# Token tile 0 leads at both changes of phase, and the convolution's inputs are computed with the activations stationary

## The chip, the cores and the metric

The kernel runs on one NeuronCore of a Trainium2 chip. The metric is the device time of one execution in microseconds (us). Its engines run apart from each other, each through its own list of instructions in order: TensorE (PE; the weight loads ahead of its matmuls are a row of their own, PEld), VectorE (DVE), ScalarE (ACT), GpSimd (POOL), and SyncE (SP), which here only issues DMA transfers. Semaphores join them.

## The reference

One residual block on 256 tokens of width 2048, batch 1, all in float32. It has three parts, each with an RMSNorm ahead and behind and with shift, scale and gate that come from a conditioning vector (9 x 2048 numbers out of a 2048 x 18432 matrix, the "ada" matrix):

```python
mod = jax.nn.silu(c) @ w_ada + b_ada                 # sh1, sc1, gt1, ..., gt3
h = modulate(rms_norm(x, g_pre[0]), sh1, sc1)
x = x + 0.5 * gt1 * rms_norm(swiglu(h, w_ffn1_gate, w_ffn1_up, w_ffn1_down), g_post[0])
h = modulate(rms_norm(x, g_pre[1]), sh2, sc2)
u_conv, q, k, v = split(h @ w_in)                    # 2048, 1024, 1024, 1024 columns
y_conv = conformer_conv(u_conv, ...)                 # a * sigmoid(g), 31 taps per channel, layer norm, silu
y_attn = diff_attention(q, k, v, ...)                # 8 heads, two softmaxes each
x = x + gt2 * rms_norm(concat([y_conv, y_attn]) @ w_out, g_post[1])
h = modulate(rms_norm(x, g_pre[2]), sh3, sc3)
x = x + 0.5 * gt3 * rms_norm(swiglu(h, w_ffn2_gate, w_ffn2_up, w_ffn2_down), g_post[2])
```

The feed-forward width is 5632. The convolution takes 2048 columns of w_in: 1024 values a and 1024 gates g.

## The kernel before

**Products.** The 256 tokens are two tiles of 128 (t = 0, 1), the 2048 channels 16 tiles (kt). A float32 product is three matmuls in the float32r format: each operand is split into a rounded part hi and a rest lo, and hi·hi, hi·lo and lo·hi are added in PSUM (mm3, L270 to L274). Weights come in blocks of 128 x 2048 floats (1 MB). `parts` (L156) loads one on the SP queue (four buffers), casts hi on ScalarE (L160) and subtracts lo on VectorE (L162); there are three hi and lo buffers. In an `s_tile` 128 x 128 pieces of the weights are stationary and 256 tokens move, so that the result has channels on the partitions; in an `m_unit` (L372) the activations are stationary (128 tokens) and 512 columns of weights move, and the result has tokens on the partitions.

**Ada chunks.** Each of the 144 chunks is 1 MB of the ada matrix: a load on the same queue and buffers, and one VectorE multiply-and-sum of 2.28 us (L183). They are strewn among the products; in ffn1 one comes per 1.1 weight blocks (EVERY1).

**Stages.** ffn1 (to about 774 us), mixing (to 1150), ffn2. Each starts with a front: `pre_norm` (L212) transposes the normalised x of both tiles for one channel tile (L218), applies scale and shift, splits, and the front adds that channel tile's products to all its open sums. In mixing the front is of class `Front` (weights stationary) and makes the first two of eight pairs (a, g) of conv channels; the other six pairs are twelve s_tiles (L638, L639). Sigmoid and gate follow (L641 to L647), then 31 taps per channel tile on VectorE (L627, L630). The taps wait in the list `fill`; each `parts` call takes up to 6 of them (TAPS), and what is left runs before the centering (`conv_done`). Then come the eight heads (q and k by s_tiles, softmax), two blocks of values, `mix_values` (L725 to L753) and `head_acts` (L760), and the four output blocks of w_out: the heads' half of the first three is done ahead while VectorE centers and normalises the conv channels (L789 to L818).

**Ends.** In the last products of each stage (`m_last`, L418) the third and fourth output blocks are run for token tile 0 first and then for tile 1. Weights of the third are split by pieces of 512 columns (`split_act`: L173 on ScalarE, L175 on VectorE). `evac` adds the partial sum (L486), ScalarE takes squares (L236), and L489 multiplies by the gate in place. `close` and `normed` then give the next stage's normalised x: L260, squares, L247.

**What sets the order.** The program only gives dependencies and hints (`behind`: not before the last matmul issued so far; `behind_dve`: the same for VectorE). The framework's scheduler puts each engine's instructions into one fixed order, and gives out the buffers (43 of 128 x 512 floats, called big).

## Time and profile before

| | |
|---|---|
| median of 3 runs | 1912.85 us (1911.74 to 1914.44) |
| the profiled execution's own time | 1911.84 us |
| its span | 1910.0 us |
| mean granted TensorE clock | 0.984 of full |
| TensorE busy | 1836.3 us (96%) |
| VectorE busy | 1423.6 us (75%) |
| ScalarE busy | 821.4 us (43%) |
| DMA | 492.58 MB, mean 258 GB/s |

Times in the views are us from the span's start. In a timeline a row has start, duration, engine, line, operation, result and operands, the count of like instructions in a row, and in brackets the idle time before it with what ended it. A matmul's duration holds the emptying of the pipeline; the rate is read from start to start. In the windows the columns are the window, its length, the busy time (and count) of PE, PEld, DVE, ACT and POOL, the granted TensorE clock (1.00 is 2.4 GHz, 0.50 is 1.2 GHz), the share of time that the DMA engines were busy, and GB/s. In the list of waits a row has the engine, the result and line that waited, what ended the wait, and then the sum, the number of waits and the longest.

### The profile page before, as it was taken

What the parts mean: (1) busy time and instruction counts of PE and PEld (TensorE: products, weight loads), DVE (VectorE), ACT (ScalarE), POOL (GpSimd) and SP (SyncE); (2) the same over time, 40 slices, a digit from 0 to 9 for tenths busy, and PEclk for the clock granted to TensorE, in tenths of its full rate; (3) what the DMA queues carried; (4) which work ended last, traced back from release to release, by engine and by line L of the source; (5) the groups of instructions that cost most, each with busy time, mean ns of one, the idle gap of its engine ahead of it and who ended that gap; (6) DMA issues with size and microseconds to landing.
All of it is one profiled execution on the core that took longest, in us unless ns stands there. A gap on an engine that the chain in (4) does not pass through costs nothing.

```text
span 1910.0 us, 22064 instructions
## 1 busy us (share of the span) xinstructions
PE 1836.3 (96%) x8944; PEld 1542.5 (81%) x8944; DVE 1423.6 (75%) x1594; ACT 821.4 (43%) x852; POOL 6.0 (0%) x49
## 2 busy tenths in 40 slices
PE   5999999999999999799998897999999999999997
PEld 3788888888888888699997686788888888888886
DVE  7789999788889888688998967854555555555455
ACT  4544445433433334643554454544344333343342
POOL 0000000000000000000000000000000000000000
PEclk9999999999999999899999898999999999999999
DMA  9888877989999998355444665865665666565552
GB/s 362 320 317 330 337 278 290 358 345 361 357 357 370 349 367 323 122 182 185 157 174 157 242 241 202 331 238 205 236 220 205 235 220 226 215 235 210 194 193 72
DMA packets 68934, 492.58 MB, mean 258 GB/s; under 512 B 7648, under 2 KB 7776, under 8 KB 9440
## 3 DMA queue, kind: packets, MB, share of 16 engines
q1 hardware_dynamic: 68832, 491.17, 69.0%
q8 instruction: 70, 1.15, 0.2%
q14 instruction: 32, 0.26, 0.0%
HBM read 489.05 MB, written 2.10 MB: 257 GB/s over the span
## 4 chain that ended last, share of the span: by engine, by line
PE 89%; DVE 5%; ACT 3%; DMA 2%; issue 0%; SPq 0%; DVEq 0%; ACTq 0%
PE ps L273 29%; PE ps L274 29%; PE ps L272 28%; DVE lo L162 2%; DMA raw<-in_wgu 2%; ACT hi L160 1%; DVE raw L183 1%; PE ps L413 1%; ACT tmp L236 1%; PE ps L312 0%; PE ps L311 0%; DMA raw<-in_wk 0%; PE ps L313 0%; PE ps L678 0%; PE ps L218 0%
## 5 line engine op out<-in xcount | busy, mean ns | idle before, releaser
L162 DVE TENSOR_TENSOR lo<-raw,hi 128x2048 fp32r<-128x2048 f32 x314 | 718.5, 2290 | 359.8 <-ACT hi L160 359.1
L160 ACT CAST hi<-raw 128x2048 fp32r<-128x2048 f32 x314 | 600.3, 1912 | 732.4 <-PE ps L274 362.0
L272 PE MATMUL ps<-hi,big 128*128 128x512 f32 x2256 | 879.2, 395 | 16.9 <-ACT big L227 11.3
L273 PE MATMUL ps<-lo,big 128*128 128x512 f32 x2256 | 884.0, 392 | 2.8 <-DVE lo L162 2.8
L274 PE MATMUL ps<-hi,big 128*128 128x512 f32 x2256 | 881.5, 392 | 2.0 <-DVE big L175 1.2
L272 PEld LDWEIGHTS ps<-hi,big 128*128 128x128 f32 x2256 | 426.1, 189 | 106.4 <-ACT big L227 12.7
L273 PEld LDWEIGHTS ps<-lo,big 128*128 128x128 f32 x2256 | 426.5, 189 | 92.5 <-DVE lo L162 6.2
L274 PEld LDWEIGHTS ps<-hi,big 128*128 128x128 f32 x2256 | 425.7, 189 | 92.5 <-DVE big L175 2.5
L183 DVE SCALAR_TENSOR_TENSOR raw<-raw,crow 128x2048 f32<-128x2048 f32 x144 | 327.7, 2283 | 0.6 <-DMA raw<-in_wada 0.5
L272 PE MATMUL ps<-big,hi 128*128 128x256 f32 x448 | 127.3, 284 | 0.0
L273 PE MATMUL ps<-big,hi 128*128 128x256 f32 x448 | 126.7, 283 | 0.0
L274 PE MATMUL ps<-big,lo 128*128 128x256 f32 x448 | 126.7, 283 | 0.0
L630 DVE SCALAR_TENSOR_TENSOR big<-big,par,big 128x256 f32<-128x256 f32 x240 | 100.1, 477 | 0.0
L272 PEld LDWEIGHTS ps<-big,hi 128*128 128x128 f32 x448 | 85.9, 192 | 0.3 <-issue 0.3
L273 PEld LDWEIGHTS ps<-big,hi 128*128 128x128 f32 x448 | 86.0, 192 | 0.0
L274 PEld LDWEIGHTS ps<-big,lo 128*128 128x128 f32 x448 | 85.9, 192 | 0.0
L397 ACT ACTIVATE tmp<-ps 128x256 f32<-128x256 f32 x64 | 24.3, 384 | 96.3 <-PE ps L274 96.3
L486 DVE TENSOR_TENSOR big<-ps,big 128x512 f32<-128x512 f32 x48 | 32.9, 691 | 31.7 <-PE ps L274 31.7
L358 DVE TENSOR_TENSOR big<-ps,big 128x512 f32<-128x512 f32 x72 | 45.2, 681 | 5.4 <-PE ps L274 5.4
L398 DVE TENSOR_TENSOR tmp<-ps,tmp 128x256 f32<-128x256 f32 x64 | 26.1, 421 | 30.9 <-ACT tmp L397 30.9
L218 PE MATMUL ps<-ident,big 128*128 128x128 f32 x96 | 19.7, 297 | 29.6 <-DVE big L247 28.7
L173 ACT CAST big<-ps 128x512 fp32r<-128x512 f32 x44 | 25.8, 585 | 38.0 <-PE ps L413 38.0
(135 smaller groups left out, 742.6 us busy)
## 6 DMA issues: line engine op xcount, KB each, us to landing
raw<-in_wada SPq DMA_DIRECT2D x144, 1024.0 KB, 6.1
raw<-in_wgu SPq DMA_DIRECT2D x116, 1024.0 KB, 5.0
raw<-in_wd SPq DMA_DIRECT2D x88, 1024.0 KB, 5.0
raw<-in_wk SPq DMA_DIRECT2D x60, 1024.0 KB, 5.5
raw<-in_wqk SPq DMA_DIRECT2D x28, 1024.0 KB, 4.8
raw<-in_wo SPq DMA_DIRECT2D x16, 1024.0 KB, 4.8
raw<-in_wv SPq DMA_DIRECT2D x8, 1024.0 KB, 4.8
raw<-in_wkc SPq DMA_DIRECT2D x4, 1024.0 KB, 5.1
```

Of the source, the lines that this page charges most:

```text
L160: nc.scalar.copy(hi, raw)
L162: ins = nc.vector.tensor_tensor(out=lo, in0=raw, in1=hi.bitcast(F32), op=ALU.subtract)
L173: nc.scalar.copy(hi[:, :w], v[:, :w])
L183: nc.vector.scalar_tensor_tensor(out=raw, in0=raw, scalar=1.0, in1=crow, op0=ALU.mult, op1=ALU.mult, accum_out=acc)
L272: nc.tensor.matmul(o, ah, bh, start=first, stop=False)
L273: nc.tensor.matmul(o, ah, bl, start=False, stop=False)
L274: last_mm[0] = nc.tensor.matmul(o, al, bh, start=False, stop=last)
L358: nc.vector.tensor_tensor(out=a[t], in0=b[t], in1=a[t], op=ALU.add)
L397: nc.scalar.activation(v[:, o], b[t][:, :S], AF.Silu)
L398: nc.vector.tensor_tensor(out=v[:, o], in0=b[t][:, S:], in1=v[:, o], op=ALU.mult)
L486: nc.vector.tensor_tensor(out=y[t][u], in0=b, in1=y[t][u], op=ALU.add)
L630: nc.vector.scalar_tensor_tensor(out=cot(c), in0=vps[c][:, j:j + S], scalar=w, in1=cot(c), op0=ALU.mult, op1=ALU.add)
```

## The change

- Conv inputs: mixing's front is now of the same class as the others (MFront, renamed Front): activations stationary, for the first two of four blocks of 512 columns (256 values a and their 256 gates). The other two blocks are m_units on a new array `wcv`. As the results have tokens on the partitions, `conv_block` copies them to SBUF, and `gated` transposes them (eight transposes a block) before sigmoid and gate. The s_tiles remain for q and k only.
- Entry: at both changes of phase pre_norm and the front run for token tile 0 alone over the first channel tiles (six in mixing, four in ffn2), then for tile 1 over the same, then for both over the rest. The first two transposes may be issued three products before the end of the last products (EARLY, LEAD).
- EVERY1 goes from 1.1 to 1.05; one `pop` more stands in the heads' loop.
- ffn's gate multiply writes into a new tile.
- Constants of mixing are set up ahead of ffn1's call.

```diff
-NF = (24, 2, 6)
+NF = (24, 4, 6)
...
-SET = (6, 2, 6)
+SET = (6, 4, 6)
 CUTS = (4, 8, 12, NK)
-EVERY1 = 1.1
+EVERY1 = 1.05
 TAPS = (3, 3, 3, 3)
...
+EARLY = 3
...
-    def pre_norm(l, xn, h, kt):
+    def pre_norm(l, xn, h, kt, ts=(0, 1)):
 
         b = bank()
-        for t in range(NT):
+        for t in ts:
             src = xn[t][kt // 4]
             o = (kt % 4) * P
             nc.tensor.transpose(b[:, t * P:(t + 1) * P], src[:, o:o + P], ident)
+        if len(h) == kt:
+            h.append(big(F32R))
+        both = h[kt]
+        o, e = ts[0] * P, (ts[-1] + 1) * P
         v = tmp()
         c = l * NK + kt
         if l and kt % 2 == 0:
-            nc.vector.tensor_scalar(out=v[:, :S], in0=b[:, :S], scalar1=gs[:, c:c + 1],
+            nc.vector.tensor_scalar(out=v[:, o:e], in0=b[:, o:e], scalar1=gs[:, c:c + 1],
                                     scalar2=sh[:, c:c + 1], op0=ALU.mult, op1=ALU.add)
         else:
-            nc.scalar.activation(v[:, :S], b[:, :S], AF.Identity, bias=sh[:, c:c + 1], scale=gs[:, c:c + 1])
-        both = big(F32R)
-        nc.scalar.copy(both[:, :S], v[:, :S])
-        last_dve[0] = nc.vector.tensor_tensor(out=both[:, S:], in0=v[:, :S], in1=both[:, :S].bitcast(F32),
-                                              op=ALU.subtract)
...
-        def step(self, kt, first, last):
+            self.banks = None
+            self.parts = {}
+
+        def step(self, kt, first, last, ts=(0, 1)):
             n = self.n
-            if first:
+            if first and ts[0] == 0:
                 self.banks = [[bank() for _ in range(NT)] for _ in range(n)]
             for j in range(n):
                 i = kt * n + j
-                if i % 4 == 0:
-                    self.parts = quarters(self.w[i // 4])
-                for t in range(NT):
-                    m_product(self.banks[j][t], t, (self.h[kt][:, :S], self.h[kt][:, S:]), self.parts[i % 4],
-                              first, last)
+                if i // 4 not in self.parts:
+                    self.parts[i // 4] = quarters(self.w[i // 4])
+                for t in ts:
+                    m_product(self.banks[j][t], t, (self.h[kt][:, :S], self.h[kt][:, S:]),
+                              self.parts[i // 4][i % 4], first, last)
...
-    def m_last(units, acts, after):
+    def m_last(units, acts, after, early=lambda: None):
...
+                    if t == NT - 1 and u == units[-1][0] and k == n - EARLY:
+                        early()
...
-                    nc.vector.tensor_tensor(out=y[t][u], in0=y[t][u], in1=gb[u], op=ALU.mult)
+                    yg = big()
+                    nc.vector.tensor_tensor(out=yg, in0=y[t][u], in1=gb[u], op=ALU.mult)
+                    y[t][u] = yg
                 if end and u == 3:
-                    xn.append(close(t, y, ss, 0.5, final))
+                    xn.append(close(t, y, ss, 0.5, nxt is None))
...
-                m_last([(u, srcs(u), None) for u in range(4 - N_LAST, 4)], acts, evac)
+                m_last([(u, srcs(u), None) for u in range(4 - N_LAST, 4)], acts, evac,
+                       (lambda: nxt.early(xn)) if nxt else (lambda: None))
...
+    class Entry:
+
+
+        def __init__(self, l, wk, late):
+            self.l, self.late = l, late
+            self.h = []
+            self.front = Front(wk, self.h, SET[l] // 2)
+            k0 = 4 * HI // self.front.n
+            self.items = [(kt, (t,)) for t in range(NT) for kt in range(k0)]
+            self.items += [(kt, (0, 1)) for kt in range(k0, NK)]
+            self.at = 0
+
+        def channels(self, xn):
+            if self.at < len(self.items):
+                kt, ts = self.items[self.at]
+                need([(3 * self.l, kt), (3 * self.l + 1, kt)], self.late)
+                pre_norm(self.l, xn, self.h, kt, ts)
+                self.at += 1
+
+        def early(self, xn):
+            for _ in range(LEAD):
+                behind(self.channels, xn)
+
+        def run(self, xn):
+            n_late = 0
+            for kt, ts in self.items:
+                self.channels(xn)
+                n_late += len(ts) / 2
+                while n_late >= LATE:
+                    n_late -= LATE
+                    behind_dve(next, self.late, None)
+                self.front.step(kt, kt == 0, kt == NK - 1, ts)
+            return self.h, self.front
...
+    mixing = Entry(1, wkc[0], bg)
+    xn = ffn(0, h, None, facts, wgu1, wd1, bg, EVERY1, mixing)
+
+
     need([(m, kt) for m in (3, 4) for kt in range(NK)], bg)
-    h, front = front_of(1, xn, wkc[0], iter(()))
+    mixing.late = iter(())
+    h, front = mixing.run(xn)
...
+    hacts = [(a[:, :S], a[:, S:]) for a in h]
+
+    def gated(cb, us):
+
+        ba, bg_ = bank(), bank()
+        for half, b in enumerate((ba, bg_)):
+            for j in range(2):
+                for t in range(NT):
+                    nc.tensor.transpose(b[:, j * S + t * P:j * S + (t + 1) * P],
+                                        us[t][:, half * S + j * P:half * S + (j + 1) * P], ident)
+        for j in range(2):
+            c = 2 * cb + j
+            js = slice(j * S, (j + 1) * S)
+            sg = tmp()
+            nc.scalar.activation(sg[:, :S], bg_[:, js], AF.Sigmoid,
+                                 bias=par[:, C_BIN + NC_ + c:C_BIN + NC_ + c + 1])
+            vp = big()[:, :S + KW - 1]
+            nc.gpsimd.memset(vp[:, 0:KW - 1], 0.0)
+            nc.vector.scalar_tensor_tensor(out=vp[:, KW - 1:], in0=ba[:, js],
+                                           scalar=par[:, C_BIN + c:C_BIN + c + 1], in1=sg[:, :S],
+                                           op0=ALU.add, op1=ALU.mult)
+            vps.append(vp)
+        fill.extend([lambda c=c_, j=j: tap(c, j) for j in range(KW) for c_ in (2 * cb, 2 * cb + 1)])
+
+    def conv_block(cb, banks):
+        us = []
+        for t in range(NT):
+            u = big()
+            nc.scalar.copy(u, banks[t])
+            us.append(u)
+        left.append(lambda: behind(gated, cb, us))
...
+    for cb in range(NC_ // 2):
+        if cb < front.n:
+            conv_block(cb, front.block(cb))
         else:
-            ba = s_tile(wqk[c - NF[1]], h)
-            bgg = s_tile(wqk[NC_ - 2 * NF[1] + c], h)
-        sg = tmp()
-        nc.scalar.activation(sg[:, :S], bgg[:, :S], AF.Sigmoid,
-                             bias=par[:, C_BIN + NC_ + c:C_BIN + NC_ + c + 1])
-        vp = big()[:, :S + KW - 1]
-        nc.gpsimd.memset(vp[:, 0:KW - 1], 0.0)
-        nc.vector.scalar_tensor_tensor(out=vp[:, KW - 1:], in0=ba[:, :S],
-                                       scalar=par[:, C_BIN + c:C_BIN + c + 1], in1=sg[:, :S],
-                                       op0=ALU.add, op1=ALU.mult)
-        vps.append(vp)
-        if c % 2:
-            fill += [lambda c=c_, j=j: tap(c, j) for j in range(KW) for c_ in (c - 1, c)]
-
-
-    w_q, w_k = wqk[2 * (NC_ - NF[1]):], wqk[2 * (NC_ - NF[1]) + NH:]
+            conv_block(cb, m_unit([wcv[kq, cb] for kq in range(4)], hacts))
...
         project(w_q, hd, 0)
+        pop()
         if hd >= 1:
             behind(softmax, hd - 1)
...
+    second = Entry(2, wk2[0], bg)
...
-        "wkc": front(1, w_in[:, :CW], w_in[:, CW:2 * CW]),
-        "wqk": s_blocks(np.concatenate([w_in[:, NF[1] * P:CW], w_in[:, CW + NF[1] * P:4 * CW]], axis=1)),
+        "wkc": m_front(1, cv[:, :NF[1] * S]),
+        "wcv": m_blocks(cv),
+        "wqk": s_blocks(w_in[:, 2 * CW:4 * CW]),
```

Line numbers change with it: L212 to L218 become L214 to L220, L160/L162 become L162/L164, L173/L175 become L175/L177, L486/L489 become L455/L459, the tap's L627/L630 become L618/L621, mm3's L272 to L274 become L276 to L278.

On VectorE, in the tail of mixing, ahead of the centering (L789) the kernel before has these rows; big_5926 holds the fourth pair of conv tiles:

```order
L630 SCALAR_TENSOR_TENSOR big_5926<-big_6696,par,big_5926 128x256
L630 SCALAR_TENSOR_TENSOR big_5926<-big_6569,par,big_5926 128x256
L175 TENSOR_TENSOR big_8446<-tmp_8442,big_8444 128x512
L630 SCALAR_TENSOR_TENSOR big_5926<-big_6696,par,big_5926 128x256
L630 SCALAR_TENSOR_TENSOR big_5926<-big_6569,par,big_5926 128x256
L630 SCALAR_TENSOR_TENSOR big_5926<-big_6696,par,big_5926 128x256
L630 SCALAR_TENSOR_TENSOR big_5926<-big_6569,par,big_5926 128x256
L630 SCALAR_TENSOR_TENSOR big_5926<-big_6696,par,big_5926 128x256
L789 TENSOR_TENSOR tmp_8542<-big_5923,big_5924 128x512
```

After the change the same place reads so; big_6010 is the fourth pair now, and the centering is L800:

```order
L177 TENSOR_TENSOR big_8129<-tmp_8125,big_8127 128x512
L621 SCALAR_TENSOR_TENSOR big_6010<-big_6456,par,big_6010 128x256
L621 SCALAR_TENSOR_TENSOR big_6010<-big_6451,par,big_6010 128x256
L177 TENSOR_TENSOR big_8140<-tmp_8136,big_8138 128x512
L621 SCALAR_TENSOR_TENSOR big_6010<-big_6456,par,big_6010 128x256
L164 TENSOR_TENSOR lo_8208<-raw_8204,hi_8206 128x2048
L621 SCALAR_TENSOR_TENSOR big_6010<-big_6451,par,big_6010 128x256
L621 SCALAR_TENSOR_TENSOR big_6010<-big_6456,par,big_6010 128x256
```

Of the taps of that pair 20 stood behind the second mix_values' reductions (L739) before; now all 62 stand behind them (L749), and 44 of these follow one another without any other row between.

Again on VectorE, at ffn1's last products, the kernel before has this; big_2524 and big_2526 are the second output block of the two token tiles, raw_5329 and raw_5347 the third block's weights:

```order
L189 TENSOR_TENSOR sh<-acc_5306,par 128x1
L175 TENSOR_TENSOR big_5337<-raw_5329,big_5335 128x512
L175 TENSOR_TENSOR big_5341<-raw_5329,big_5339 128x512
L175 TENSOR_TENSOR big_5345<-raw_5329,big_5343 128x512
L486 TENSOR_TENSOR big_2524<-ps_5237,big_2524 128x512
L486 TENSOR_TENSOR big_2526<-ps_5238,big_2526 128x512
L175 TENSOR_TENSOR big_5351<-raw_5347,big_5349 128x512
L489 TENSOR_TENSOR big_2524<-big_2524,ps_5232 128x512
L175 TENSOR_TENSOR big_5355<-raw_5347,big_5353 128x512
```

After the change (big_2540 and big_2542 are that output block, raw_5369 the weights):

```order
L455 TENSOR_TENSOR big_2540<-ps_5275,big_2540 128x512
L455 TENSOR_TENSOR big_2542<-ps_5276,big_2542 128x512
L459 TENSOR_TENSOR big_5350<-big_2540,ps_5270 128x512
L459 TENSOR_TENSOR big_5355<-big_2542,ps_5270 128x512
L177 TENSOR_TENSOR big_5373<-raw_5369,big_5371 128x512
L177 TENSOR_TENSOR big_5377<-raw_5369,big_5375 128x512
L177 TENSOR_TENSOR big_5381<-raw_5369,big_5379 128x512
L164 TENSOR_TENSOR lo_5411<-raw_5407,hi_5409 128x2048
L177 TENSOR_TENSOR big_5385<-raw_5369,big_5383 128x512
```

The subtractions of the split (L175, now L177) stood ahead of the addition that waits for the second block, and stand behind it and its gate multiply now.

On TensorE, at the first change of phase, the kernel before goes from the last product straight to the transposes of both tiles (big_5462 is the normalised x of tile 0, big_5553 of tile 1):

```order
L274 MATMUL ps_5366<-hi_5375,big_5175 128x512
L218 MATMUL ps_5577<-ident,big_5462 128x128
L218 MATMUL ps_5585<-ident,big_5462 128x128
L218 MATMUL ps_5593<-ident,big_5462 128x128
L218 MATMUL ps_5577<-ident,big_5553 128x128
L218 MATMUL ps_5585<-ident,big_5553 128x128
L218 MATMUL ps_5593<-ident,big_5553 128x128
L311 MATMUL ps_5601<-big_5582,hi_5605 128x256
```

After the change, behind three transposes and two channel tiles of tile 0, it reads (big_5506 is of tile 0, big_5611 of tile 1):

```order
L276 MATMUL ps_5628<-hi_5632,big_5565 128x512
L277 MATMUL ps_5628<-lo_5634,big_5565 128x512
L278 MATMUL ps_5628<-hi_5632,big_5565 128x512
L220 MATMUL ps_5655<-ident,big_5506 128x128
L220 MATMUL ps_5674<-ident,big_5506 128x128
L220 MATMUL ps_5687<-ident,big_5611 128x128
L220 MATMUL ps_5705<-ident,big_5611 128x128
L220 MATMUL ps_5717<-ident,big_5611 128x128
L276 MATMUL ps_5626<-hi_5664,big_5621 128x512
L277 MATMUL ps_5626<-lo_5666,big_5621 128x512
```

Of a run of tile 0's matmuls, the first twelve now stand ahead of tile 1's transposes and the rest behind three of them.

## Rows read from the trace of the kernel before

**Rows 1.** The page's first part: busy us (share of the span) and instructions

```profile
PE 1836.3 (96%) x8944; PEld 1542.5 (81%) x8944; DVE 1423.6 (75%) x1594; ACT 821.4 (43%) x852; POOL 6.0 (0%) x49
```

**Rows 2.** What TensorE waited for: total us, times, longest

```profile
PE ps L218 <- DVE big L247: 28.7, 5, 10.9
...
PE ps L760 <- DVE tmp L750: 5.8, 1, 5.8
...
PE ps L272 <- ACT big L173: 3.4, 1, 3.4
...
PE ps L273 <- DVE lo L162: 2.8, 4, 1.3
```

**Rows 3.** Busy time by window; columns as in the table above

```profile
520.00:550.00 30.00, 29.22 (x129) 23.44 (x128) 26.69 (x22) 10.82 (x8) 0.00 (x0) 1.00 0.97 355
...
774.00:790.00 16.00, 3.75 (x15) 2.87 (x15) 13.32 (x27) 11.08 (x26) 0.00 (x0) 0.60 0.36 132
...
820.00:880.00 60.00, 60.00 (x503) 60.00 (x502) 54.90 (x88) 21.83 (x16) 0.00 (x0) 1.00 0.49 176
...
920.00:1000.00 80.00, 80.00 (x626) 75.09 (x624) 77.59 (x161) 39.84 (x81) 2.84 (x25) 1.00 0.46 165
```

**Rows 4.** Timeline of TensorE in values: start, duration, engine, line, operation

```profile
1007.82 0.39 PE L273 MATMUL ps<-lo,big 128*128 128x512 f32 x1
...
1010.77 0.39 PE L274 MATMUL ps<-hi,big 128*128 128x512 f32 x1
```

**Rows 5.** Timeline of TensorE, eight transposes of a gate row

```profile
751.19 1.04 PE L131 MATMUL ps<-ident,gt 128*128 128x128 f32 x8
```

**Rows 6.** Timeline of TensorE at the first change of phase

```profile
780.44 0.90 PE L218 MATMUL ps<-ident,big 128*128 128x128 f32 x3 [6.35 <-DVE big L247]
...
786.44 0.90 PE L218 MATMUL ps<-ident,big 128*128 128x128 f32 x3 [5.11 <-DVE big L247]
...
788.14 0.79 PE L311 MATMUL ps<-big,hi 128*128 128x256 f32 x2 [0.79 <-ACT big L227]
```

**Rows 7.** Timeline of VectorE there

```profile
786.96 0.99 DVE L222 TENSOR_SCALAR tmp<-ps,gs,sh 128x256 f32<-128x256 f32 x2 [0.17 <-PE ps L218]
...
788.12 1.10 DVE L228 TENSOR_TENSOR big<-tmp,big 128x256 fp32r<-128x256 f32 x3 [0.17 <-ACT big L227]
```

**Rows 8.** Costliest groups of the page: count, busy us, mean ns, idle before

```profile
L162 DVE TENSOR_TENSOR lo<-raw,hi 128x2048 fp32r<-128x2048 f32 x314 | 718.5, 2290 | 359.8 <-ACT hi L160 359.1
...
L183 DVE SCALAR_TENSOR_TENSOR raw<-raw,crow 128x2048 f32<-128x2048 f32 x144 | 327.7, 2283 | 0.6 <-DMA raw<-in_wada 0.5
```

**Rows 9.** Timeline of ScalarE at ffn1's last products

```profile
744.32 2.18 ACT L173 CAST big<-raw 128x512 fp32r<-128x512 f32 x4 [1.85 <-DMA raw<-in_wd]
...
751.44 0.63 ACT L236 ACTIVATE tmp<-big 128x512 f32<-128x512 f32 x1 [3.53 <-DVE big L486]
```

**Rows 10.** What VectorE waited for in 1043 to 1089

```profile
DVE lo L162 <- ACT hi L160: 1.8, 3, 1.1
```

**Rows 11.** Timeline of VectorE in the tail of mixing

```profile
1042.92 1.27 DVE L739 TENSOR_REDUCE rs<-tmp 128x4 f32<-128x512 f32 x2
...
1055.63 2.06 DVE L630 SCALAR_TENSOR_TENSOR big<-big,par,big 128x256 f32<-128x256 f32 x5
...
1088.35 3.25 DVE L818 SCALAR_TENSOR_TENSOR big<-big,par,tmp 128x256 f32<-128x256 f32 x8
```

**Rows 12.** Timelines of ScalarE and VectorE at ffn2's last products

```profile
1858.39 2.18 ACT L173 CAST big<-raw 128x512 fp32r<-128x512 f32 x4
...
1876.76 1.37 DVE L486 TENSOR_TENSOR big<-ps,big 128x512 f32<-128x512 f32 x2 [0.48 <-PE ps L274]
```

**Rows 13.** Timeline of TensorE at the second change of phase

```profile
1150.02 0.49 PE L218 MATMUL ps<-ident,big 128*128 128x128 f32 x3
...
1161.41 0.90 PE L218 MATMUL ps<-ident,big 128*128 128x128 f32 x3 [10.90 <-DVE big L247]
...
1163.11 0.80 PE L272 MATMUL ps<-hi,big 128*128 128x512 f32 x1 [0.80 <-ACT big L227]
```

More of the change, by code (lines that the diff above doesn't have):

```diff
@@ L556, in first_front @@
         return h, facts
-    def front_of(l, xn, wk, late):
-        h = []
-        front = Front(wk, h, SET[l]) if l == 1 else MFront(wk, h, SET[l] // 2)
-        n_late = 0
-        for i in range(NK + LEAD):
-            if i < NK:
-                need([(3 * l, i), (3 * l + 1, i)], late)
-                pre_norm(l, xn, h, i)
-            n_late += 1
-            while n_late >= LATE:
-                n_late -= LATE
-                behind_dve(next, late, None)
-            if i >= LEAD:
-                front.step(i - LEAD, i == LEAD, i == NK + LEAD - 1)
-        return h, front
+    class Entry:
[26 more added lines that the diff above has]
+            return self.h, self.front
     xn = []
@@ L718, in values @@
     def values(u, hooks):
-        hacts = [(h[kt][:, :S], h[kt][:, S:]) for kt in range(NK)]
         banks = m_unit([wv[kq, u] for kq in range(4)], hacts, hooks)
@@ L861, in block_kernel @@
                 mix_evac(u, t, open_[u][t])
-    m_last([(u, of_conv(u), open_[u]) for u in range(4 - N_LAST, 4)], conv_acts, mix_evac)
-    h, front = front_of(2, xn, wk2[0], bg)
-    ffn(2, h, front, {}, wgu2, wd2, ada_of([(8, kt) for kt in range(NK)]), 6, True)
+    m_last([(u, of_conv(u), open_[u]) for u in range(4 - N_LAST, 4)], conv_acts, mix_evac,
+           lambda: second.early(xn))
+    h, front = second.run(xn)
+    ffn(2, h, front, {}, wgu2, wd2, ada_of([(8, kt) for kt in range(NK)]), 6, None)
 def _layout(i):
```

58 lines of the change are left out of this document (9 added, 49 removed).

## The prediction

> **What bounds the kernel now.** I read the page first, then the list of TensorE's waits, then busy time and clock by windows, then each engine's timeline around every wait of over 1 us. TensorE is busy for 1836.3 of 1910.0 us [rows 1], so 73.7 us are all that a better order of work can win, and most of it stands in a few places [rows 2]: pre_norm's transposes wait 28.7 us for normalised activations (at the start and at the two changes of phase), one wait of 5.8 us is for mix_values, one of 3.4 us for the convolution's normalised channels. VectorE (75% in the page's table) is second, and for stretches it decides: its rows are in a fixed order, so a stage is late when a row that TensorE needs stands behind many that nobody waits for. In ffn1 it is DMA: in 520-550 its share is 0.97 at 355 GB/s, with TensorE idle for 0.8 of 30 us [rows 3].
>
> **The change, term by term.** Durations are of the profiled execution: 1911.84 us, of which the span is 1910.0; that is 1.0 us below the median of the runs, 1912.85.
>
> *1. Conv inputs with the activations stationary.* Removed are 768 matmuls of 256 columns. In 820-880, which holds nothing else, TensorE is full with 503 of them, 60.0 / 503 = 0.119 us each [rows 3]; some records can be missing, so I take 0.120: 92.2 us. Added are 384 of 512 columns; 13 steps lie between 1007.82 and 1010.77, 0.2265 each [rows 4]: 87.0. That saves 5.2. Added too are 32 transposes; eight take 1.04 us with the last one's tail [rows 5], so 32 are at most 4.2, and I take 3.9. Net: -1.3. Eight copies from PSUM to SBUF come on ScalarE, four of them ahead of one weight cast; four casts of that shape take 2.18 us [rows 12], and I let TensorE wait for all of it once: +2.2. From below that is 0 (the next weights are cast in time), from above 4.4 (both blocks). The pads on POOL are as many as before.
>
> The Trainium skill (TensorE: Matmul & The Clock Gate, "Wait — 56ns, not 53.3ns?") speaks against the 5.2: it gives a warm matmul its columns over the clock and a fixed 2.5 ns or so, so that half as many matmuls of twice the columns save an estimated 1 us, and the net would be near +3. The rows don't agree: 2 x 0.119 is 0.238 against 0.227, so about 12 ns per matmul are saved here [rows 3, 4].
>
> *2. First change of phase.* Before, TensorE idles 6.35 us to three transposes of tile 0 at 780.44, 5.11 us to tile 1's at 786.44, and the first matmul is at 788.14 [rows 6]; the clock granted in 774-790 is 0.60 [rows 3]. In the new order two of tile 0's six leading channel tiles (12 matmuls, 12 x 0.2265 = 2.7 us) come before a group of five transposes, of which the last three read tile 1, and TensorE can't pass them. Tile 1's own chain on VectorE gets no shorter, and tile 0's scale-and-shift rows (0.99 and 1.10 us of such work [rows 7]) are now ahead of it: 2.1 us later. 2.7 - 2.1: -0.6. Bounds: -6 (the 5.1 us between the tiles filled, and the clock back sooner) and +2 (the 12 matmuls hide behind nothing that matters, and the chain is later all the same).
>
> *3. EVERY1.* Four more ada chunks go into ffn1: on the SP queue, two weight loads in a row without a chunk between them fall from seven places to three. A chunk costs VectorE 2.28 us [rows 8], which has room, and DMA 1 MB at 355 GB/s, 2.95 us [rows 3], which hardly has. From below 0: weights' lead covers it, since waits for lo cost TensorE only 2.8 us in four places now [rows 2]. From above 9: three of the four, once the lead is gone. I take one chunk, +2.9, as these four waits are nearer to the lower end.
>
> *4. ffn1's last products.* Now the casts for the split weights start at 744.32, ahead of the squares at 751.44 [rows 9], whose input is there when the block before ends (I call that U, 751.2). In the new order both squares on ScalarE and four rows on VectorE that follow U stand ahead of all eight casts. Counted on from U with these durations: squares to 1.9; three casts of 0.51; a weight cast of 1.9; one; another weight cast; four, to 9.9. VectorE's subtractions, two lo rows of 2.2 us among them, end at 12.8. TensorE, at three matmuls (0.68 us) a product, then ends tile 0's part at U + 18, where before it was U + 12.7. That is +5.3 if the weights are all there. Bounds +2 (only the first cast's wait) and +6; I take +4.5, since DMA gains on TensorE while it waits.
>
> *5. The tail of mixing, the largest term.* The fourth pair of conv channels is gated later, so its taps start later. Behind the second mix_values' first reduction VectorE had 20 of the 62 taps of that pair; it now has all 62, still ahead of the centering. Five taps take 2.06 us with the last one's tail, 0.396 from start to start [rows 11]: 42 x 0.396 = +16.6. From that reduction (1042.92) to the scaling of the conv channels (1088.35) [rows 11], the new order has one ada chunk fewer (-2.2) and one lo row fewer (-2.2), and the 1.8 us of waits for weight casts [rows 10] go: +10.4. Cover there is none: TensorE waits 3.4 us for just these channels already [rows 2], so what VectorE is late is late at the end. Bounds: +5 (loads that come earlier let the heads' stage run ahead by half of it) and +13.
>
> *6. Second change of phase.* Before: idle for 10.9 us between three transposes of tile 0 at 1150.02 and those of tile 1 at 1161.41, first matmul 1163.11 [rows 13]. Tile 0 is ready early, as the first three show. In the new order two transposes stand among the last products, and 18 matmuls (two of four leading channel tiles, 4.1 us) run before three transposes of tile 1 block. Restart at 1161.5 by the same chain: 1.6 + 4.1 = 5.7, and 0.6 for the slow start, as the clock comes back while TensorE would have idled: -6.3. Bounds: -9 (all 36 matmuls, 8.2 us, go first) and -3 (tile 1 gets 3 us later by the rows of tile 0).
>
> *7. The end.* ffn2 closes with the same products. Before, the first four casts ran at 1858.39, and the block that the squares wait for ended at 1876.76 [rows 12]. After, all eight stand behind both squares: the first ends at U + 2.7, TensorE starts there and meets no later wait, as a product takes 0.68 us against about 0.5 a cast and 0.6 a subtraction. +2.7; bounds 0 and +4.
>
> The gate multiply into a new tile is as long as in place; it only lets VectorE's next rows go without waiting for the squares. The constants' loads (SP) and masks (POOL) move under ffn1, where both queues have room for them: nothing.
>
> Sum: -1.3 + 2.2 - 0.6 + 2.9 + 4.5 + 10.4 - 6.3 + 2.7 = +14.5, and 1911.84 + 14.5 = 1926 us.
>
> **Rivals.**
> *A. Tile 0's lead works in full: faster.* If tile 1's transposes never hold TensorE, it fills the 5.1 us at the first change, and 8.2 at the second, and saves some 3 and 1 us of half-speed clock; with -1.3 for the conv inputs and half of term 5 (+5) hidden in the heads' stage, and 0 for the rest, that is -13.6: 1898. For it: the idle time is there [rows 6, 13]. Against: the order has the blocking transposes, and VectorE is busy for 77.6 of 80 us in 920-1000 [rows 3]. It decides if the taps before the second mix_values come to 20 more than I count.
> *B. Only the tail and the second change count: no change.* +10.4 - 6.3 - 1.3 and nothing else: +2.8, 1915. For it: the lead of the weights, and a ScalarE that the page's table has busy for 43% of the span. Against: terms 4 and 7 follow from rows that are in a fixed order.
> *C. DMA decides in ffn1: much slower.* +9 in term 3, +5.3 in term 4: 1911.84 + 14.5 + 6.9 = 1933. For it: the share of 0.97. Against: four waits only.
> *D. The form of the matmul saves nothing.* Without the 5.2 us it is 1931. Against: rows 3 and 4, as above. That is where the Trainium skill's rule on a matmul's fixed cost would put it, nearly.
>
> **How the numbers follow.** My forecast has 0.55, A 0.20, B 0.12, C 0.09, D 0.04. What a measurement of this kernel can tell from no change is about 0.2%, 3.8 us. Faster: A and a little of B, 0.22. Within: most of B, 0.10. Slower: the rest, 0.68. The likeliest's own range, by the larger bounds of terms 3, 5 and 6 taken crosswise, is 1918 to 1934; half of A lies below 1903, and C's far side above 1935, so 1903 to 1935 is the range.
>
> **What would show it.** Term 5: a wait of TensorE of over 10 us inside the blocks of w_out, and VectorE in taps for over 20 us behind the second mix_values. Terms 2 and 6: a stop of TensorE after 12 matmuls of the new phase, and after 18, each ended by the normalised rows of tile 1. Terms 4 and 7: waits for the split's casts in the last products. Term 3: more than four waits for lo in 400-700. The prediction is wrong if TensorE's wait for the conv channels stays near 3.4 us, or if tile 1 no longer ends a wait at the changes of phase.

## The result

The changed kernel takes 1922.74 us (median of 4 runs, 1920.49 to 1925.65), the kernel before 1913.14 beside it: a ratio of 1.0051, 95% interval [1.0034, 1.0069]. It is slower by some 9.6 us, where 14.5 were forecast. The profiled execution took 1922.9 us, its span is 1921.1. The first part of its page, and then its list of TensorE's waits (engine, result and line, what ended the wait: us in total, times, longest):

```profile
PE 1840.3 (96%) x8592; PEld 1523.9 (79%) x8592; DVE 1424.4 (74%) x1609; ACT 828.4 (43%) x875; POOL 6.0 (0%) x49
```

```profile
PE ps L220 <- DVE big L251: 22.4, 5, 7.5
PE ps L794 <- DVE tmp L802: 11.3, 1, 11.3
...
PE ps L276 <- ACT big L175: 7.7, 4, 4.3
PE ps L277 <- DVE lo L164: 5.4, 10, 1.9
...
PE ps L770 <- DVE tmp L760: 3.9, 1, 3.9
```

TensorE is busy for 4.0 us more than before, with fewer matmuls, and idle for 7.1 us more.

Against [rows 2] the waits for normalised activations fall by 6.3 us: by 8.7 at the two changes of phase, while the start of the program has 2.3 more. (The start spreads without any edit: the first transpose comes at 12.8 us in the trace of the kernel before, and at 15.0 in that of e11_before_taps4 below, which differs from it in the taps of mixing alone.) The wait for mix_values falls by 1.9. New is the wait of 11.3 us for the centering's sum (L802). The split's casts (L175) stop TensorE four times instead of once: the one of before is for the conv channels, and is 4.3 us now where it was 3.4; 2.0 and 1.2 us stand in the last products of ffn1 and ffn2, and 0.2 ahead of w_out. Lo rows stop it ten times instead of four, six times in 400 to 700, where it was twice.

The first change of phase, TensorE's timeline after (start, duration, engine, line; in brackets the idle time before):

```profile
785.80 0.39 PE L278 MATMUL ps<-hi,big 128*128 128x512 f32 x1
792.23 0.90 PE L220 MATMUL ps<-ident,big 128*128 128x128 f32 x3 [6.04 <-DVE big L251]
794.32 0.80 PE L276 MATMUL ps<-hi,big 128*128 128x512 f32 x1 [1.19 <-ACT big L232]
...
797.12 0.68 PE L276 MATMUL ps<-hi,big 128*128 128x512 f32 x1
797.63 0.40 PE L277 MATMUL ps<-lo,big 128*128 128x512 f32 x1
...
800.92 0.55 PE L220 MATMUL ps<-ident,big 128*128 128x128 f32 x3 [1.74 <-DVE big L251]
801.95 0.50 PE L276 MATMUL ps<-hi,big 128*128 128x512 f32 x1 [0.48 <-ACT big L232]
```

Where [rows 6] had two waits of 6.35 and 5.11 us and the first product at 788.14, 14.4 us after the last one of ffn1, it now is there 8.5 us after. Tile 1's three transposes still stop TensorE after twelve matmuls, but for 1.74 us, and by then the clock is back: the step from start to start is 0.43 us up to 797.1 and 0.23 from 797.6. In the kernel before, the half-speed steps came behind the restart and lasted from 788.14 to 794.2 (matmuls of 256 columns, 0.21 us from start to start and then 0.12):

```profile
793.68 0.41 PE L313 MATMUL ps<-big,lo 128*128 128x256 f32 x1
...
794.39 0.28 PE L312 MATMUL ps<-big,hi 128*128 128x256 f32 x1
794.51 0.29 PE L313 MATMUL ps<-big,lo 128*128 128x256 f32 x1
```

In the windows after (columns as in [rows 3]), the clock granted over 16 us from ffn1's end is 0.79, where [rows 3] had 0.60, and the second row shows no stop in the second half of the conv inputs:

```profile
784.00:800.00 16.00, 7.95 (x28) 5.51 (x26) 12.58 (x25) 11.76 (x28) 0.61 (x5) 0.79 0.38 132
845.00:895.00 50.00, 50.00 (x245) 42.12 (x244) 41.90 (x70) 24.68 (x23) 0.00 (x0) 1.00 0.51 186
```

The second change, as [rows 13]:

```profile
1169.38 0.39 PE L278 MATMUL ps<-hi,big 128*128 128x512 f32 x1
1175.66 0.90 PE L220 MATMUL ps<-ident,big 128*128 128x128 f32 x3 [5.90 <-DVE big L251]
1176.70 0.79 PE L276 MATMUL ps<-hi,big 128*128 128x512 f32 x1
```

The 10.9 us have become 5.9, and eighteen matmuls of the new phase are done by 1169.38.

The tail of mixing, VectorE after (the columns are the same), as [rows 11]:

```profile
1049.55 1.27 DVE L749 TENSOR_REDUCE rs<-tmp 128x4 f32<-128x512 f32 x2
...
1062.69 17.51 DVE L621 SCALAR_TENSOR_TENSOR big<-big,par,big 128x256 f32<-128x256 f32 x44
1080.13 0.67 DVE L800 TENSOR_TENSOR tmp<-big,big 128x512 f32<-128x512 f32 x1
...
1104.20 3.25 DVE L829 SCALAR_TENSOR_TENSOR big<-big,par,tmp 128x256 f32<-128x256 f32 x8
```

From the reduction to the scaling of the conv channels it takes 54.65 us, where it took 45.43; 44 of the 62 taps lie in one piece of 17.5 us, and TensorE's 11.3 us of waiting end with the centering behind them. TensorE's first product of conv channels, before and after, and the wait that follows it:

```profile
1090.73 0.80 PE L272 MATMUL ps<-hi,big 128*128 128x512 f32 x1 [3.43 <-ACT big L173]
...
1094.47 1.22 PE L274 MATMUL ps<-hi,big 128*128 128x512 f32 x2 [1.24 <-DVE big L175]
```

```profile
1107.77 0.50 PE L276 MATMUL ps<-hi,big 128*128 128x512 f32 x1 [4.28 <-ACT big L175]
...
1110.32 1.22 PE L278 MATMUL ps<-hi,big 128*128 128x512 f32 x2 [0.37 <-DVE big L177]
```

ffn1's last products, ScalarE after, as [rows 9]:

```profile
760.05 0.63 ACT L240 ACTIVATE tmp<-big 128x512 f32<-128x512 f32 x1 [8.45 <-DVE big L455]
...
761.36 1.64 ACT L175 CAST big<-raw 128x512 fp32r<-128x512 f32 x3
762.91 1.90 ACT L162 CAST hi<-raw 128x2048 fp32r<-128x2048 f32 x1
764.71 0.62 ACT L175 CAST big<-raw 128x512 fp32r<-128x512 f32 x1
765.23 1.90 ACT L162 CAST hi<-raw 128x2048 fp32r<-128x2048 f32 x1
767.03 2.18 ACT L175 CAST big<-raw 128x512 fp32r<-128x512 f32 x4
```

ScalarE is idle for 8.45 us and only then, behind the squares, begins the casts that it did ahead of them before. TensorE waits 2.04 us for the first of them, and 1.4 us behind that wait its granted clock falls to 0.50 for 3.4 us, a second cost of some 1.7 (an estimate: half of the stretch). The first row is its timeline, the others are windows:

```profile
762.01 0.50 PE L276 MATMUL ps<-big,big 128*128 128x512 f32 x1 [2.04 <-ACT big L175]
```

```profile
763.50:766.80 3.30, 3.30 (x9) 2.56 (x9) 2.35 (x2) 3.30 (x3) 0.00 (x0) 0.50 0.01 5
767.00:775.00 8.00, 8.00 (x37) 6.61 (x36) 5.44 (x8) 4.12 (x6) 0.00 (x0) 1.00 0.84 333
```

### The profile page after: what moved, and what is told of

It reads as the page before. It is cut to its first block, busy times and chain, and to the rows that moved or that the text cites. A ratio compares the mean times of both kernels' runs of the same rounds, so it can differ in the third digit from the quotient of the medians.

```text
span 1921.1 us, 21411 instructions
## 1 busy us (share of the span) xinstructions
PE 1840.3 (96%) x8592; PEld 1523.9 (79%) x8592; DVE 1424.4 (74%) x1609; ACT 828.4 (43%) x875; POOL 6.0 (0%) x49
## 4 chain that ended last, share of the span: by engine, by line
PE 78%; DVE 9%; DMA 7%; ACT 4%; issue 1%; SPq 0%; DVEq 0%; ACTq 0%
PE ps L277 25%; PE ps L278 25%; PE ps L276 25%; DMA raw<-in_wgu 5%; DVE lo L164 4%; ACT hi L162 3%; DVE raw L185 2%; DMA raw<-in_wd 2%; DVE big L621 1%; PE ps L380 1%; ACT tmp L240 1%; DMA x<-in_x 0%; PE ps L220 0%; PE ps L689 0%; DMA raw<-in_wk 0%
## 5 line engine op out<-in xcount | busy, mean ns | idle before, releaser
L164 DVE TENSOR_TENSOR lo<-raw,hi 128x2048 fp32r<-128x2048 f32 x314 | 718.5, 2290 | 384.9 <-ACT hi L162 381.2
L276 PE MATMUL ps<-hi,big 128*128 128x512 f32 x2384 | 930.9, 396 | 20.1 <-ACT big L232 10.9
L277 PE MATMUL ps<-lo,big 128*128 128x512 f32 x2384 | 937.2, 393 | 5.8 <-DVE lo L164 5.4
L278 PE MATMUL ps<-hi,big 128*128 128x512 f32 x2384 | 931.5, 392 | 0.4 <-DVE big L177 0.4
L162 ACT CAST hi<-raw 128x2048 fp32r<-128x2048 f32 x314 | 600.2, 1912 | 752.1 <-PE ps L278 407.9
L276 PEld LDWEIGHTS ps<-hi,big 128*128 128x128 f32 x2384 | 451.0, 189 | 115.4 <-ACT big L232 13.0
L277 PEld LDWEIGHTS ps<-lo,big 128*128 128x128 f32 x2384 | 451.6, 189 | 103.6 <-DVE lo L164 13.0
L278 PEld LDWEIGHTS ps<-hi,big 128*128 128x128 f32 x2384 | 449.5, 189 | 96.9 <-DVE big L177 2.1
L621 DVE SCALAR_TENSOR_TENSOR big<-big,par,big 128x256 f32<-128x256 f32 x240 | 99.7, 476 | 0.0
L276 PE MATMUL ps<-big,hi 128*128 128x256 f32 x256 | 73.2, 286 | 0.0
L277 PE MATMUL ps<-big,hi 128*128 128x256 f32 x256 | 72.5, 283 | 0.0
L278 PE MATMUL ps<-big,lo 128*128 128x256 f32 x256 | 72.5, 283 | 0.0
L276 PEld LDWEIGHTS ps<-big,hi 128*128 128x128 f32 x256 | 49.1, 192 | 0.4 <-issue 0.3
L277 PEld LDWEIGHTS ps<-big,hi 128*128 128x128 f32 x256 | 49.1, 192 | 0.0
L278 PEld LDWEIGHTS ps<-big,lo 128*128 128x128 f32 x256 | 49.1, 192 | 0.0
L455 DVE TENSOR_TENSOR big<-ps,big 128x512 f32<-128x512 f32 x48 | 32.5, 689 | 21.5 <-PE ps L278 21.3
L231 ACT ACTIVATE tmp<-ps,sh,gs 128x256 f32<-128x256 f32 (+1 forms) x37 | 19.6, 534 | 54.9 <-PE ps L220 36.3
L220 PE MATMUL ps<-ident,big 128*128 128x128 f32 x96 | 20.1, 289 | 22.8 <-DVE big L251 22.4
```

Source lines behind the costliest of these rows:

```text
L162: nc.scalar.copy(hi, raw)
L164: ins = nc.vector.tensor_tensor(out=lo, in0=raw, in1=hi.bitcast(F32), op=ALU.subtract)
L220: nc.tensor.transpose(b[:, t * P:(t + 1) * P], src[:, o:o + P], ident)
L276: nc.tensor.matmul(o, ah, bh, start=first, stop=False)
L277: nc.tensor.matmul(o, ah, bl, start=False, stop=False)
L278: last_mm[0] = nc.tensor.matmul(o, al, bh, start=False, stop=last)
```

## The experiments

Ratios are to the kernel before, run beside each on the same chip; the changed kernel's is 1.0051. Microseconds "by the ratios" are the difference of two ratios times 1913 us. To see where a kernel differs, I took from each profiled execution the times of six landmarks and of the end, and subtracted the kernel before's. The table shows what each stage gained (-) or lost (+) against it, in us. The landmarks: the addition L486 (L455 after) for tile 1 of ffn1's first output block (741.0 before; this row lies one block ahead of U), the last such addition of ffn1 (776.3), the first and the last softmax product (903.9, 993.9), the first multiply with the gate in mixing (1107.4) and the last (1151.6), ffn2's first addition (1517.5), the end (1910.0).

| kernel | ratio, 95% interval | to ffn1's 1st block | ffn1's last products | change 1 and conv inputs | heads | values, tail | rest of mixing | change 2, ffn2's first products | rest |
|---|---|---|---|---|---|---|---|---|---|
| changed | 1.0051 [1.0034, 1.0069] | +7.3 | +4.3 | -5.0 | 0 | +7.2 | +1.3 | -4.4 | +0.2 |
| e1_taps4 | 0.9989 [0.9978, 1.0] | +7.9 | +3.0 | -2.2 | +0.9 | -5.0 | +0.6 | -3.5 | +0.2 |
| e2_every | 1.003 [1.002, 1.0041] | -0.3 | +2.2 | -4.8 | 0 | +7.5 | +1.3 | -1.3 | +0.2 |
| e3_inplace | 1.0024 [1.0011, 1.0036] | +2.8 | -0.2 | -3.0 | 0 | +8.4 | +1.3 | -3.8 | -0.6 |
| e4_three | 0.9959 [0.9942, 0.9975] | +0.8 | 0 | -4.6 | +0.9 | -5.7 | +1.1 | -0.5 | -0.6 |
| e5_nolead | 1.0067 [1.0053, 1.008] | +5.0 | +4.1 | -0.5 | 0 | +8.3 | +0.9 | -2.4 | +0.2 |
| e6_form | 1.004 [1.0026, 1.0055] | +2.4 | +0.1 | -2.4 | 0 | +7.8 | +0.9 | +4.6 | -0.6 |
| e7_behind | 0.9973 [0.9963, 0.9983] | +3.4 | 0 | -1.2 | +0.9 | -5.2 | +0.7 | -0.1 | -0.6 |
| e8_chunks | 0.9945 [0.9931, 0.9959] | -1.4 | 0 | +2.8 | +0.9 | -5.0 | +1.6 | -6.3 | -0.6 |
| e9_best | 0.9938 [0.9922, 0.9954] | +7.7 | +0.7 | -1.9 | +0.9 | -4.8 | +0.7 | -6.3 | -0.6 |
| e10_nolead3 | 0.9991 [0.9981, 1.0] | +1.3 | +0.1 | -2.8 | +0.9 | -5.1 | +0.2 | +6.2 | -0.6 |
| e11_before_taps4 | 0.999 [0.998, 1.0001] | +4.1 | 0 | -0.4 | +2.5 | -4.2 | 0 | +1.6 | -0.3 |

The first column must be read with care: e2, e4, e6, e7, e8, e9, e10 and e11 have ffn1's old pace, and still spread from -1.4 to +7.7. One profile can't price anything there; the ratios of several runs can.

**The three costs, one by one.**

```diff
-TAPS = (3, 3, 3, 3)
+TAPS = (4, 4, 4, 4)
```

> The changed kernel with one number other: up to eight taps a weight load instead of six, in every stage of mixing, so that no tap of the fourth pair is left behind the second mix_values (62 before this edit). Theory (the taps on VectorE set the start of the conv channels' products): TensorE's wait of 11.3 us for the centering's mean goes to under 2 us, the conv channels' first product comes 13 to 17 us sooner than at 1107.8, and the kernel is 8 to 14 us faster than the changed one, at about 1911. Rival (VectorE is 97% busy in the heads' stage, so eight taps per load make the lo rows late): TensorE gets waits for lo between 895 and 1050 of 5 us or more, and the gain is under 4 us.

The theory held. The ratio falls from 1.0051 to 0.9989, 11.9 us, and the tail from +7.2 to -5.0; the conv channels' first product comes at 1094.4, 13.3 us sooner. TensorE's wait at the mean is gone from its list. The rival's mechanism is there, but small; TensorE's waits in 895-1050, all of them:

```profile
PE ps L277 <- DVE lo L164: 1.6, 2, 1.0
```

```diff
-EVERY1 = 1.05
+EVERY1 = 1.1
```

> The changed kernel with ada chunks in ffn1 at the old pace (EVERY1 1.1 for 1.05), four chunks fewer there. Theory (DMA decides in ffn1, and what was gained in lead by two weight loads in a row is gone): the second last output block of ffn1 ends 5 to 7 us sooner, the waits for lo fall from ten to about four, and the kernel is about 6 us faster than the changed one. Rival (the 6 us that the trace of the changed kernel shows up to that block are its later start of 2.6 us and chance, or the four chunks cost the same wherever they are): under 2 us.

4.0 us by the ratios, less than the theory and more than the rival; the two intervals overlap, so the gain is likely, and its size open. Waits for lo fall from ten to seven, in 400 to 700 from six to two. The four chunks are not gone: they come in ffn2's front, where TensorE now waits for lo rows (its timeline, only rows with a wait):

```profile
1209.72 0.50 PE L277 MATMUL ps<-lo,big 128*128 128x512 f32 x1 [2.16 <-DVE lo L164]
1220.31 1.66 PE L276 MATMUL ps<-hi,big 128*128 128x512 f32 x6 [0.31 <-ACT hi L162]
1222.63 0.50 PE L277 MATMUL ps<-lo,big 128*128 128x512 f32 x1 [0.66 <-DVE lo L164]
1229.66 0.50 PE L277 MATMUL ps<-lo,big 128*128 128x512 f32 x1 [1.31 <-DVE lo L164]
```

That stage's gain shrinks from -4.4 to -1.3: three of the microseconds that ffn1 no longer pays are paid there. Read the other way, three of the 4.4 us that the changed kernel gains in this stage come from the chunks that went to ffn1, and not from tile 0's lead.

```diff
-                    yg = big()
-                    nc.vector.tensor_tensor(out=yg, in0=y[t][u], in1=gb[u], op=ALU.mult)
-                    y[t][u] = yg
+                    nc.vector.tensor_tensor(out=y[t][u], in0=y[t][u], in1=gb[u], op=ALU.mult)
```

> The changed kernel with the gate multiply of both FFNs back in place. Theory (the new tile is what lets the squares and the gate rows go ahead of the split's casts in the last products): the wait of 2.0 us at ffn1's last products goes and those products end some 3.5 us sooner, at ffn2's some 1.4 us are won and 1.1 lost, as the last multiply then waits for its square again; 3 to 5 us faster than the changed kernel. Rival (the order comes from elsewhere, or TensorE's waits there only move): within 1 us of the changed kernel.

5.2 us by the ratios, just above the theory. ffn1's last products lose nothing any more (-0.2 for +4.3), the end goes from +0.2 to -0.6, and casts of the split stop TensorE once, as before, for the conv channels (4.28 us). So it was the new tile that let the rows of the block before overtake the split; the rival is out.

> All three edits together: eight taps a load, the old pace of ada chunks, the gate multiply in place. Theory (the three costs stand in different stages, one behind the other, and add up): 10 to 13 for the taps, 6 for the chunks, 4 for the gate, about 1900 to 1904, faster than the kernel before by 9 to 13 us, which is what tile 0's lead and the conv inputs' form are worth. Rival (part of these waits hide each other, or the heads' stage pays for the taps): at or above the kernel before, 1912 or more.

1905.33 us, ratio 0.9959: the three win 17.6 us together by the ratios, against 21.1 one by one. They nearly add up; that is 1 us short of the theory, and the kernel is then 0.4% faster than the one before.

**Tile 0's lead, and the form.**

```diff
-            k0 = 4 * HI // self.front.n
+            k0 = 0
...
-            for _ in range(LEAD):
-                behind(self.channels, xn)
+            pass
...
             n_late = 0
+            for _ in range(LEAD):
+                self.channels(xn)
             for kt, ts in self.items:
```

> The changed kernel without tile 0's lead: at both changes of phase pre_norm and the front run for both tiles together, two channel tiles ahead, as in the kernel before; nothing is issued early. Theory (the lead is worth what the trace shows: some 4.7 us at the first change and 4.2 at the second, since matmuls run while tile 1 is being normalised and the clock is back sooner): 7 to 10 us slower than the changed kernel, at about 1931. Rival (the lead gains nothing, since tile 1's chain is later by what stands in front of it): within 2 us of the changed kernel.

0.16%, 3 us by the ratios, and the intervals overlap: between theory and rival, nearer to the rival. By stages the lead is worth 4.5 us at the first change and 2.0 at the second.

> The three edits together, without tile 0's lead at the changes of phase. Theory (the lead is worth what the stages of the traces show, 2 to 4.5 us at the first change and 2 to 5 at the second): 5 to 8 us slower than the three edits with the lead, about 1911. Rival (the lead gains only what the medians with and without it gave in the changed kernel, 3 us): 1908 or less.

The same edit on the three together: 0.9991 against 0.9959, 6.1 us by the ratios, as the theory had it. By stages it is 1.8 at the first change and 6.7 at the second.

The two sizes at the first change (4.5 and 1.8) differ by the granted clock. Behind the restart TensorE goes at half speed for 6.0 us in e5_nolead and for 3.5 in e10_nolead3. And in e4_three, as in five others of the eight traces with the lead, the clock falls once more about where the stop for tile 1 ends, for 3.4 us, which it does not in the changed kernel's trace. Windows of e4_three:

```profile
786.20:789.50 3.30, 1.22 (x7) 0.77 (x5) 2.58 (x9) 3.07 (x10) 0.12 (x1) 1.00 0.00 0
789.60:792.90 3.30, 3.13 (x8) 2.32 (x9) 2.56 (x10) 2.75 (x10) 0.00 (x0) 0.50 0.00 0
793.00:800.00 7.00, 7.00 (x33) 5.74 (x32) 0.21 (x1) 0.76 (x2) 0.00 (x0) 1.00 0.00 0
```

The two sizes at the second (2.0 and 6.7) go with the pace of the chunks: at the old pace, four chunks more lie in ffn2's front. e10_nolead3, and e6_form below, wait 3.27 and 3.14 us for a weight cast there, with 7 us of half speed behind it; e5_nolead has no such wait, and with the lead it is 0.7 us at most. The kernel before has as many chunks in ffn2 as they, no lead, and no such wait either. So the 6.7 us are not the lead's alone; against the kernel before, e4_three gains just 0.5 in this stage.

> The conv inputs' new form alone: the changed kernel without tile 0's lead, with the old pace of ada chunks and the gate multiply in place, so that against the kernel before only the activations are stationary in the conv inputs and the pair's taps come later. Theory (the products save 1.3 us net, the taps behind the second mix_values cost 8 to 10): 5 to 10 us slower than the kernel before, with a wait of over 10 us for the centering. Rival (the form itself is dear: copies, transposes and PSUM held longer, beside the taps): more than 12 us slower, with waits of TensorE inside 795 to 890. Rival (the taps cost only because other things were late): within 3 us of the kernel before.

1.004, 7.7 us slower: the first theory. Its tail loses 7.8, as much as the whole; TensorE's wait for the centering is 11.0 us. Beside that the conv inputs gain 2.4 and ffn2's front loses 4.6, with this wait:

```profile
1227.87 2.37 PE L276 MATMUL ps<-hi,big 128*128 128x512 f32 x6 [3.14 <-ACT hi L162]
```

The changed kernel's window of 845-895, shown above, has TensorE busy throughout, so no copy or transpose stops it there. And with the taps fitting, the new form (e10_nolead3, 0.9991) and the old one (e11_before_taps4, 0.999) are equal in the whole, though not stage by stage.

```diff
                     behind_dve(next, self.late, None)
                 self.front.step(kt, kt == 0, kt == NK - 1, ts)
+                if hold:
+                    behind(self.channels, xn)
```

(`hold` is true where the next transposes are of tile 1 alone; they are then not issued ahead of the step.)

> The three edits together (eight taps a load, the old pace of ada chunks, the gate in place), and each transpose of tile 1 at a change of phase not before the product two steps later of tile 0, so that 30 (mixing) and 27 (ffn2) of tile 0's 36 matmuls stand ahead of tile 1's first transpose, where there were 12 and 18. Theory (what stops TensorE after 12 and 18 matmuls is only the place of tile 1's transposes): the stop of 6.3 us at the second change becomes under 4 and that of 2 us at the first under 0.5, 3 to 4 us faster than the three edits alone. Rival (tile 1's first channel tiles now start later, and each of their steps waits for its own scale and split): the waits come back as several of 1 us between tile 1's steps, within 1 us of the three edits alone.

Neither: 0.9973 against 0.9959, no gain and perhaps a loss. At the first change waits of 2.8, 1.1 and 0.7 us for tile rows' casts and subtractions take the place of the 2.2 us of e4_three. The stop at the second change is 6.95 us now, and it is not tile 1's transposes that stand there. TensorE, then VectorE and ScalarE around it:

```profile
1160.15 0.79 PE L276 MATMUL ps<-hi,big 128*128 128x512 f32 x1 [6.95 <-ACT big L232]
```

```profile
1154.22 2.74 DVE L264 SCALAR_TENSOR_TENSOR x<-big,ri,x 128x512 f32<-128x512 f32 x4
1156.88 0.40 DVE L228 TENSOR_SCALAR tmp<-ps,gs,sh 128x128 f32<-128x128 f32 x1
```

```profile
1157.02 0.61 ACT L240 ACTIVATE tmp<-x 128x512 f32<-128x512 f32 x1
1157.54 0.18 ACT L240 ACTIVATION_READ_ACCUMULATOR tmp<-x 128x1 f32 x1
1157.63 0.44 ACT L231 ACTIVATE tmp<-ps,sh,gs 128x128 f32<-128x128 f32 x1
1158.14 0.20 ACT L209 ACTIVATE sq<-rs 128x1 f32<-128x1 f32 x1
1158.57 1.33 ACT L249 ACTIVATE big<-x,ri 128x512 f32<-128x512 f32 x2 [0.23 <-DVE ri L211]
1159.81 0.48 ACT L232 CAST big<-tmp 128x128 fp32r<-128x128 f32 x2
```

The product waits for tile 0's third channel tile. Its scale-and-shift (L228) stands on VectorE behind tile 1's additions (L264), and ends at 1157.28; its cast (L232) then stands on ScalarE behind tile 1's squares (L240) and normalised copies (L249), until 1159.81. So VectorE's order holds it for the first 3.7 us of the stop, and ScalarE's for 2.5 more. Tile 0's products can't go ahead of tile 1's norm, because on these two engines tile 0's rows don't. This was not in my theory: taking TensorE's obstacle away leaves another one at the same time.

**A place for the chunks.**

```diff
-    mixing.late = iter(())
+    mixing.late = islice(bg, 6)
```

> As the one with tile 1's transposes held back, and six ada chunks moved out of ffn2's front into mixing's front, where VectorE is busy for 26 of 45 us and DMA has a share of 0.40. Theory (with the old pace, ffn1 no longer pays for the four chunks, but ffn2's front does: waits for lo of 2.4, 1.1 and 1.7 us there; a chunk is cheap only where both VectorE and DMA have room): those waits go, 2 to 4 us faster than without the move. Rival (in mixing's front the chunks stand in the way of the scale-and-shift rows and of the first weights): waits of the same size in 780 to 840, no gain or a loss of up to 4 us.

0.9945 against 0.9973: 5.4 us by the ratios, more than the theory. Change 2 gains 6.2, change 1 loses 4.0 (one wait of 4.0 us for a lo row there), so both mechanisms act and the stages leave 2.2; the other part of the difference is not explained by the profile.

> The three edits together (eight taps a load, old pace of ada chunks, gate in place) and six ada chunks moved out of ffn2's front into mixing's front; tile 1's transposes stay where the changed kernel has them. Theory (the chunks' move wins some 2 to 5 us as it did with tile 1's transposes held back, and holding those back lost 2 to 4): 1899 to 1902, 0.7% under the kernel before. Rival (the chunks' wait of 4.3 us in mixing's front is as dear as the ones in ffn2's front, and the difference of the two runs was chance): 1905, as the three edits alone.

1900.6 us, 0.9938: the fastest here, 0.62% under the kernel before; the theory's size. Its interval and that of e4_three overlap, so the chunks' own share is likely and not shown. In the profiled execution ffn1 alone is 7.7 us longer; it took 1908.2 us, the median is 1900.6.

> The kernel before the change with eight taps a load; none is then left behind the second mix_values, where there were 20. Theory (a tap on that path costs 0.2 to 0.3 us at the conv channels' first product, whatever the form of the conv inputs; 62 of them were worth 12.5): about 4 us faster than the kernel before. Rival (with the taps gone the conv channels' products wait for something else at nearly the same time, so 20 taps were free): within 1.5 us of the kernel before.

0.1%, about 2 us, between theory and rival; the interval goes from the theory's 4 us to none, so it decides neither. The tail gains 4.2 us by stages, so the 20 taps were not free there; the heads give 2.5 back in waits for lo.

## Why the prediction was right, and where its terms were off

The time (1922.74) is in the likeliest case's own range of 1918 to 1934, the sign is right, and the main term is the main one. That the sum came so near is partly luck: in the profiled execution ffn1 up to its first output block (which spreads by itself, as said) took 7.3 us more for a forecast of 2.9, the first change and the conv inputs 5.0 less for +0.3, and these misses nearly cancel.

- *Term 5, the tail: the mechanism and nearly the size.* The first product of conv channels came 10.4 us later against the rest (1107.77 for 1090.73, with 6.6 us of delay before the heads), as the sum said; on VectorE the stretch that it was read from is 9.2 us longer. Three of these are regained up to the first gate multiply: the wait that follows is 0.37 us for 1.24, and TensorE's half-speed steps end 3.8 us after the first product, for 7.3 before. That was not in the term. 42 taps more are +7.2 to +8.4 in the table. By the letter, the mark of being wrong is near: the wait for the conv channels themselves is 4.28 us, not far from 3.4. The delay stands in the wait ahead of it, for the centering, which was the mark for being right (over 10 us; it is 11.3).
- *Term 2, the first change, was the term mis-sized most:* -0.6 against a stage of -5.0, of which the lead has 1.8 to 4.5. The restart was forecast well (14.4 + 2.1 = 16.5 us after ffn1's last product, measured 16.15). What failed is "2.7 - 2.1": it priced twelve matmuls at full clock as the whole gain. But TensorE starts at the half-speed level after the idle time in either kernel, and stays there for 6.1 us before and 3.2 now. Now that stretch falls on the twelve matmuls, which begin 7.6 us before tile 1's, and at the restart the clock is whole. The prediction has this in its bound of -6 and in rival A (3 us), and not in the term. With it, 2.7 and 3 less the 1.7 by which the restart is later give about -4, an estimate. (In six of the eight traces with the lead the clock falls once more, as said for e4_three.)
- *Term 1:* the form itself, -1.3, can't be told from nothing by the ratios, and agrees with the traces: from the first product behind the change to the first softmax product it is 115.8 us before and 114.2 in e5_nolead, with half-speed stretches of the same length (6.1 and 6.0 us). The 13 steps of [rows 4] are 0.2269 us each and not 0.2265, which changes the term by 0.1. The copies' +2.2 didn't come: TensorE has no wait between 802 and 1055.
- *Term 3:* +2.9; 4.0 by the ratios for the whole kernel; in the traces three more were paid in ffn1 and won back in ffn2's front. Its mark, more than four waits for lo in 400-700, was met: six.
- *Term 4 and 7:* +4.5 and +2.7; +2.2 to +4.3 in the traces with the new tile, and +0.8 at the end. The +4.3 is the forecast's size, but not its way: the wait for the casts costs about 2.2 us, the lower bound, and the rest is mostly the half speed behind it, which e1_taps4 (+3.0) does not have after the same wait. TensorE does wait at ffn2's last products (1.45 us from start to start), and the last multiply, which no longer waits for its square, gives most of that back; I had put that at nothing.
- *Term 6:* -6.3; the stop shrank as forecast, from 10.9 to 5.9 us, but the stage is -4.4, and -1.3 and -0.5 with the chunks at the old pace (e2_every, e4_three). The 0.6 for the slow start did not come: behind the restart TensorE is at half speed for 3.2 us in both kernels.

Rival A fell by the reason given against it, and by one that I had not seen, the order on VectorE and ScalarE. C is out by its size: +9 in term 3, where the ratios give 4.0. D is out: without the saving the conv inputs would be 3.9 us longer by term 1's numbers, and in e5_nolead they are 1.6 us shorter.

## What to carry to other kernels

Work that only fills gaps (the taps) needs a count of what is left at the point where somebody waits for all of it; a form that makes its input later moves that work behind the point without changing one duration. A new buffer that takes a wait away can cost more than the wait, because a scheduler then lets the freed rows go ahead of rows that are more urgent. A lead of one tile over another has to hold on every engine of the chain, here on VectorE and ScalarE too, not on TensorE alone. And a short wait of TensorE can cost more than its length: three traces have the wait of 2.0 us in ffn1's last products, and in two of them (the changed kernel and e5_nolead) the granted clock was 0.50 for 3.4 us behind it.

## What was not expected of the hardware

With the same pace of ada chunks ffn1 took from -1.4 to +7.7 us against the kernel before up to its first output block, in eight profiled executions; DMA's share in their window of 400 to 740 is 0.93 to 0.95. The slower ones moved less in a microsecond there (361 GB/s at -1.4, 353 at +7.7); what slows them is not shown. Several runs beside each other were needed for differences of 4 us.
